# Layer 0's value products: sums of x by adding DMAs, sums of the weights on VectorE, later gathers, projections 8 steps ahead

## The chip, the cores and the metric

The kernel runs on one core of a Trainium2 chip. The metric is the device time of one execution in microseconds; the time of a kernel is the median of its timed runs. A profile is one further execution, recorded by the hardware profiler, with a time of its own.

The engines, as the profile abbreviates them: PE is TensorE (matmuls; PEld its weight loads), DVE is VectorE, ACT is ScalarE, POOL is GpSimd, SP is SyncE, which here only issues DMAs. Each engine executes its instructions in an order that is fixed when the kernel is built. An instruction that must wait holds up all behind it on its engine.

## The reference

Two layers of a decoder trunk over 1024 tokens of width 1024, in float32. Layer 0 mixes tokens by differential attention, layer 1 by forgetting attention; each is followed by a gated MLP with a short convolution, and residuals with LayerNorm. The change touches the attention of layer 0 only:

```python
q, k, v = jnp.split(x @ w_qkv, 3, axis=-1)           # 1024 x 1024 each
q = apply_rotary(q.reshape(B, S, H, 2, d), ...)      # 8 heads x 2 components x 64, 16 of 64 rotated
k = apply_rotary(k.reshape(B, S, H, 2, d), ...)
v = v.reshape(B, S, H, 2 * d)
# per block of 128 queries
s = einsum('bhcqd,bhckd->bhcqk', qb, k) * d ** -0.5
p = masked_softmax(s, causal_mask)
a = p[:, :, 0] - lam * p[:, :, 1]
o = einsum('bhqk,bhkd->bqhd', a, v)
o = rms_norm(o, subln_g) * (1.0 - lambda_init)
# all blocks together, then @ w_o
```

## The kernel before

**Number format.** Every large product is made of three matmuls (`mm3`, L104 to L106): each operand is cut into a high part and a remainder, and high x high, high x remainder and remainder x high are summed. `split` makes the two parts: an ACT copy (L91) for the high part and a DVE subtraction (L95) for the remainder.

**Loads and first projections.** `first_pair_rotary` loads x transposed (`in_xT`: 128 partitions x 8 blocks of the contraction x 1024 tokens) and the first two weight slabs, computes the rotary tables (their DMAs go through POOL's queue), and projects the query and key of head pair 0, first for tokens 0 to 511 (c = 0), then for 512 to 1023 (c = 1). `value_weights` (L379) loads all of the value weights, 8 tiles of 512 KB, on SP. `exp_table` loads ACT's table for the exponential in a section of its own.

**The value products.** `values_upfront` computes all values at once, x (1024 x 1024) times a 1024 x 1024 weight, by Winograd's form of Strassen's method: x and weight are taken as 2 x 2 blocks (halves of the tokens or features, `lo` and `hi`, and halves of the contraction, `k` and `H + k` with H = 4), and seven half-size products replace eight. Products 1, 2 and 4 use blocks of x as they are; 5, 7, 6 and 3 need sums of blocks:

- product 5: x(k, hi) + x(H+k, hi)
- product 6: that minus x(k, lo)
- product 7: x(k, lo) - x(k, hi)
- product 3: x(H+k, lo) minus the operand of product 6

The weights need sums of the same kind for 5, 6, 7 and 4. Before the change DVE makes the sums of x and POOL those of the weights (all by the helper `sub`, L411). Raw blocks of x come in by `load` (L403) into the tile `xs`, one per k, and `x1`, which has only two buffers of tag `wst`, so that the third and fourth are loaded after product 6 has used the first and second. `make(m, k)` produces the operands of product m for block k; `product` runs 4 row groups j of 12 matmuls per two k; `drain` combines PSUM results and stores the values to DRAM (L476), from where `load_values` (L533) reads them for each head pair. The products run in passes (1, 2), (5, 6), (7, 3), (4), in each pass k by k with the two products in turn, the last two k together. Operands are made up to `V_AHEAD` = 4 ahead.

**Rotation of pair 0.** The rotated rows are gathered by 12 small DMAs per half of the tokens (`gather`, L630 and L632) into the tile `rt`, multiplied by the tables (`turn`, L639 to L641, DVE), written back (L645) and then split (`halves`, with moves L273). All DMAs but the rotary tables' are issued by SP. `after(n, f)` defers f by n pulses; a pulse comes with every three matmuls of a product. Before the change the first half is gathered as soon as its projection is copied out, and its turn is called ahead of the second half's results.

**The attention loop.** For each of 8 head pairs (p), 16 score jobs run (two components j for each block qt of 128 queries: two groups of matmuls L682/L683, a masked minimum on DVE L685, the exponential on ACT L708, the normalisation L713, the combination on DVE L718), followed by transposes (L1544), value products and the norm of the heads (`diff_values`: squares summed by a matmul with ones, L743). Between jobs `step` advances the projection of later pairs by one block of the contraction, three matmuls per step. A pair's projection (`project_rotary`) is 4 quarters of 8 steps: (query, c=0), (key, c=0), (query, c=1), (key, c=1). `SHIFT` sets how far the projections run ahead: pair 0 advances them by 32 + SHIFT steps, pairs 1 to 5 by 32, pair 6 by 32 - SHIFT, and pair 7 has the output projection's first 64 steps instead. `ahead` (L113) loads a weight slab into a `wst` buffer, `ready` cuts it; the second component's exponentials use the `wst` buffers too, from qt = 4 on, and the free half of `rt` for qt < 4. `D_EV`, `D_ROT` and `D_CUT` are the delays of evacuation, turn and cut behind a quarter, in pulses.

Of the kernel before, what the change touches and what calls it, by code (L numbers as in the profile page):

```python
# [15 lines left out]
ALU = mybir.AluOpType  # L16
# [22 lines left out]
D_EV, D_ROT, D_CUT, D_TV = 1, (9, 10), ((14, 14), (18, 20)), 1  # L39
V_ROT, V_CUT, V_G, V_AHEAD = 20, (12, 32), 2, 4  # L40
SHIFT, D_VAL = 16, 10
# [17 lines left out]
class Trunk:  # L59
# [281 lines left out]
    def first_pair_rotary(self, t):  # L341
# [13 lines left out]
        for c in range(2):  # L355
# [3 lines left out]
            if c:  # L359
                self.turn(dst, r, 0)  # L360
# [4 lines left out]
            self.gather(dst, r, c)  # L365
        self.lam_exp()
        self.after(V_ROT, self.turn, dst, r, 1)
# [5 lines left out]
    def value_weights(self):  # L373
# [6 lines left out]
        return tiles[::2], tiles[1::2]  # L380

    def values_upfront(self, raw, cur):
# [6 lines left out]
        (g, u), H = raw, KT // 2  # L389
# [8 lines left out]
        xs, x1, ops = {}, {}, {}  # L398
        self.flip, n_s = False, 0

        def load(d, k, ns, t):
            d[k] = t
            nc.sync.dma_start(t.rearrange("p (k n) -> p k n", k=2), self.i["xT"][:, k:k + H + 1:H, ns])  # L403

        for k in range(H):
            load(xs, k, lo, self.tmp(pool=self.tt, tag="pt") if k < 3 else self.tmp(pool=self.pp, tag="p"))
            if k < 2:
                load(x1, k, hi, self.tmp(pool=self.wp, tag="wst", bufs=2))
# [4 lines left out]

        def make(m, k):
            nonlocal n_s
            gp, ve = nc.gpsimd, nc.vector
            if m == 5:
                sub(gp, g[k][:, lo], g[k][:, hi], g[k][:, lo])
                sub(ve, x1[k][:, hi], x1[k][:, lo], x1[k][:, hi], ALU.add)
                src = x1[k][:, hi]  # L420
            elif m == 6:
                sub(gp, g[k][:, lo], u[k][:, hi], g[k][:, lo])
                src = sub(ve, x1[k][:, hi], x1[k][:, hi], xs[k][:, lo])
            elif m == 7:
                sub(gp, g[k][:, hi], u[k][:, hi], g[k][:, hi])
                src = xs[k][:, lo]
            elif m == 3:
                src = xs[k][:, hi]
            elif m == 4:
                sub(gp, u[k][:, lo], u[k][:, lo], g[k][:, lo])  # L430
# [5 lines left out]
            else:  # L436
# [3 lines left out]
                self.split(*x, src)  # L440
                if m == 6:
                    sub(ve, xs[k][:, hi], xs[k][:, hi], src)
                    sub(ve, xs[k][:, lo], xs[k][:, lo], x1.pop(k)[:, lo])
                    if k < 2:
                        load(x1, k + 2, hi, self.tmp(pool=self.wp, tag="wst", bufs=2))
# [1322 lines left out]
```

## Time and profile before

| what | us |
|---|---|
| timed runs: median (lowest to highest of 3) | 2474.3 (2473.54 to 2485.29) |
| the profiled execution's own time | 2467.94 |
| its span | 2466.1 |
| mean granted clock of PE | 0.993 |
| the value products' matmuls (`wo`), first to last | 37.3 to 137.5 |
| windows of the head pairs, by their first scores: pair 0 | 138 to 185 |
| pair 1 | 185 to 232.5 |
| pair 6 | 413 to 465.2 |

How to read the rows of the profile: a row of a timeline has the start and the duration in us, engine, line, operation, output <- inputs, and in brackets the idle time before it with what ended it. A row of grouped instructions ends in busy us, mean ns of one, and idle time before them. A row of windows has the stretch, its length, the engine's busy time with its count of instructions, then for all engines alike PE's granted clock (1.00 is full speed), the mean busy share of the 16 DMA engines, and GB/s. A row of waits has total us, times, longest us. A row of DMA issues has the count, KB each, and the median us from issue to landing.

### The profile page before, as it was taken

The page shows a single profiled execution, that of the slowest core. Times are in us where ns is not written, and L with a number is a line of the kernel's source. Part 1 is how long each engine was busy: PE and PEld are TensorE (multiplying, and loading weights), DVE is VectorE, ACT ScalarE, POOL GpSimd, SP SyncE. Part 2 cuts the span into 40 slices and gives each one's busy share as a digit, 9 for nine tenths or more (in the row PEclk, how much of TensorE's full clock was granted, in tenths as well). Part 3 has the DMA queues.
Part 4 walks back from the last instruction along what each step waited for, and adds up shares of the span by engine and source line. Part 5 has one row for each costly group of instructions (what it writes and reads, how often), then busy time and mean ns, then how long its engine had stood idle before and what let it go on. Part 6 is the DMA issues. An engine that isn't in the chain of part 4 may idle for free.

```text
span 2466.1 us, 33746 instructions
## 1 busy us (share of the span) xinstructions
PE 2403.4 (97%) x11691; PEld 1998.3 (81%) x11691; DVE 1930.4 (78%) x3763; ACT 1312.5 (53%) x2516; POOL 163.7 (7%) x337
## 2 busy tenths in 40 slices
PE   7799999999999999999999999999999999999998
PEld 6588888778888888888778888888888888888886
DVE  5778888889867667887858777778898667668977
ACT  3467788766544444544535555555565444445444
POOL 4101111001000000000101000000010000000000
PEclk9899999999999999999999999999999999999999
DMA  6454335532322223975232222225223222328851
GB/s 198 150 164 130 107 98 144 162 107 94 103 77 77 94 86 98 337 253 171 87 99 62 67 66 65 65 74 171 78 86 111 78 77 78 97 97 318 270 170 69
DMA packets 140467, 304.38 MB, mean 123 GB/s; under 512 B 19116, under 2 KB 43564, under 8 KB 140296
## 3 DMA queue, kind: packets, MB, share of 16 engines
q1 hardware_dynamic: 139496, 300.32, 38.1%
q8 instruction: 92, 1.51, 0.3%
q0 software_dynamic: 800, 1.90, 0.2%
q14 instruction: 79, 0.65, 0.1%
HBM read 201.03 MB, written 67.57 MB: 109 GB/s over the span
## 4 chain that ended last, share of the span: by engine, by line
PE 78%; DVE 9%; ACT 6%; DMA 4%; issue 2%; SPq 1%; POOL 0%; DVEq 0%; ACTq 0%; POOLq 0%
PE m L104 19%; PE m L106 18%; PE m L105 18%; PE s L104 4%; PE s L105 4%; PE s L106 4%; PE m L1544 3%; PE s L683 2%; PE s L682 2%; PE m L1570 1%; PE m L1569 1%; DVE s L685 1%; DMA q<-q 1%; DMA t<-od 1%; DMA pt<-in_wd 1%
## 5 line engine op out<-in xcount | busy, mean ns | idle before, releaser
L104 PE MATMUL m<-xh,wh 128*128 128x512 f32 x640 | 266.7, 417 | 12.5 <-ACT xh L91 10.6
L104 PE MATMUL m<-xh,wo 128*128 128x512 f32 x656 | 255.9, 390 | 1.1 <-DVE xl L95 0.9
L106 PE MATMUL m<-xh,wo 128*128 128x512 f32 x656 | 255.6, 390 | 0.0
L105 PE MATMUL m<-xl,wo 128*128 128x512 f32 x656 | 255.6, 390 | 0.0
L106 PE MATMUL m<-xh,wl 128*128 128x512 f32 x640 | 253.8, 397 | 0.0
L105 PE MATMUL m<-xl,wh 128*128 128x512 f32 x640 | 252.4, 394 | 0.5 <-DVE xl L95 0.5
L91 ACT ACTIVATE wo<-wg 128x512 fp32r<-128x512 f32 x168 | 106.3, 633 | 223.7 <-PE m L106 215.8
L685 DVE CUSTOM_DVE_ANT_0 s<-s,mask 128x128 f32<-128x128 f32 (+7 forms) x256 | 194.0, 761 | 35.8 <-PE s L683 34.8
L104 PE MATMUL m<-q,wo 128*128 128x512 f32 x472 | 184.2, 390 | 0.0
L106 PE MATMUL m<-q,wo 128*128 128x512 f32 x472 | 183.9, 390 | 0.0
L105 PE MATMUL m<-q,wo 128*128 128x512 f32 x472 | 183.9, 390 | 0.0
L91 ACT ACTIVATE pt<-m 128x512 fp32r<-128x512 f32 (+1 forms) x240 | 128.6, 554 | 101.6 <-PE m L1544 67.4
L95 DVE TENSOR_TENSOR pt<-m,pt 128x512 fp32r<-128x512 f32 (+1 forms) x240 | 148.6, 633 | 23.3 <-ACT pt L91 20.5
L91 ACT ACTIVATE wo<-t 128x512 fp32r<-128x512 f32 x135 | 84.7, 627 | 142.3 <-PE m L106 134.8
L677 POOL CAST qz<-q 64x128 fp32r<-64x128 f32 x256 | 97.7, 383 | 847.5 <-PE s L683 774.5
L104 PEld LDWEIGHTS m<-xh,wh 128*128 128x128 f32 x640 | 121.6, 190 | 32.5 <-ACT xh L91 11.0
L95 DVE TENSOR_TENSOR wo<-wg,wo 128x512 fp32r<-128x512 f32 x168 | 115.5, 688 | 38.8 <-ACT wo L91 37.9
L104 PEld LDWEIGHTS m<-xh,wo 128*128 128x128 f32 x656 | 123.2, 188 | 27.2 <-PE m L1136 1.4
L105 PEld LDWEIGHTS m<-xl,wo 128*128 128x128 f32 x656 | 123.2, 188 | 25.5
L106 PEld LDWEIGHTS m<-xh,wo 128*128 128x128 f32 x656 | 123.2, 188 | 25.5
L106 PEld LDWEIGHTS m<-xh,wl 128*128 128x128 f32 x640 | 120.8, 189 | 26.1 <-DVE wl L95 0.6
L682 PE MATMUL s<-q,q 128*128 128x512 f32 (+3 forms) x384 | 134.0, 350 | 6.3 <-ACT p L708 4.2
(392 smaller groups left out, 6337.0 us busy)
## 6 DMA issues: line engine op xcount, KB each, us to landing
t<-in_wi SPq DMA_DIRECT2D x44, 512.0 KB
ha<-ad SPq DMA_DIRECT2D x88, 256.0 KB
wg<-in_wi SPq DMA_DIRECT2D x42, 512.0 KB
ad<-t SPq DMA_DIRECT2D x42, 512.0 KB
wst<-in_w SPq DMA_DIRECT2D x38, 512.0 KB
q<-q SPq DMA_DIRECT2D x128, 128.0 KB
pt<-in_wd SPq DMA_DIRECT2D x24, 512.0 KB
hb<-in_wd SPq DMA_DIRECT2D x44, 256.0 KB
```

Of the source, the lines that this page charges most:

```text
L91: i = nc.scalar.activation(hi, src, AF.Copy, scale=1.0 if scale is None else scale)
L95: nc.vector.tensor_tensor(lo, src, hi.bitcast(F32), op=ALU.subtract)
L104: mm(out, wh, xh, start=start, stop=False)
L105: mm(out, wh, xl, start=False, stop=False)
L106: mm(out, wl, xh, start=False, stop=stop)
L677: nc.gpsimd.tensor_copy(qz[r:r + 64, :], q[r:r + 64, qt * P:qt * P + P])
L682: nc.tensor.matmul(sb[:, ks], q[:, qt * P:qt * P + P], kd[:, ks], start=True, stop=False)
L683: nc.tensor.matmul(sb[:, ks], qz[rows], kl[rows, ks], start=False, stop=True)
L685: nc.vector.tensor_tensor_reduce(sb[:, :ln], sb[:, :ln], self.mask[:, S - ln:], 1.0, BIG, ALU.add, ALU.min, mn)
L1544: nc.tensor.transpose(tb[:, w:w + P], self.pts[q][:, kt * P:kt * P + P], k.ident)
L1569: mm(o, self.v[0][:, vs], h, start=first, stop=False)
L1570: mm(o, self.v[0][:, vs], l, start=False, stop=last)
```

## The change

- `value_weights` also loads the sums of x. For each k it makes three sums in place: a plain load by SP of one block, and then adding DMAs by POOL's queue, which read a block of `in_xT` from DRAM and add it onto the tile. `x1` lo gets (k, hi) + (H+k, hi), `x2` gets (k, hi) + (H+k, hi) + (k, lo), `x1` hi gets (k, lo) + (k, hi). These are 12 loads and 16 adds, 256 KB each. The loads are pinned behind the eight weight loads on SP, ahead of all gathers. Once product 6 has split its `x2`, one more adding DMA puts (H+k, lo) onto it for product 3 (4 in all).
- So that all sums of x are additions, the half of x for tokens 512 to 1023 is taken with its sign turned. Products 5, 6, 7 and 4 take their weights' sums with the sign that this asks for, and the drains for that half of the tokens scale by -1.
- The sums of the weights move from POOL to DVE. DVE's sums of x go.
- Pair 0's rotation is deferred: the gathers of the halves to 1 and 23 pulses, the turns to 20 and 42, the cuts to 31 and 54 (before: gathers at once, turns ahead of the second half's results and at 20, cuts at 12 and 32).
- In the loop `SHIFT` goes from 16 to 8; a quarter's gather is issued per operand; turns and cuts get new delays; the loads and cuts of weight slabs move to other quarters; in the last pair the second component's exponentials take other buffers; the matmul with ones is called a pulse later.

```diff
@@ -36,9 +36,9 @@
 
 AHEAD = 6
 EARLY = 8
-D_EV, D_ROT, D_CUT, D_TV = 1, (9, 10), ((14, 14), (18, 20)), 1
-V_ROT, V_CUT, V_G, V_AHEAD = 20, (12, 32), 2, 4
-SHIFT, D_VAL = 16, 10
+D_EV, D_ROT, D_CUT, D_TV = 1, (8, 8), ((14, 14), (14, 14)), 1
+V_ROT, V_GA, V_CUT, V_G, V_AHEAD = (20, 42), 19, (31, 54), 2, 4
+SHIFT, D_VAL = 8, 10
 W_CUT = 3
 D_V = 5, 9
 LAG, VLAG, W_C = 1, 0, 2
@@ -356,15 +356,15 @@
             ps = [self.mbank() for _ in range(2)]
             for _ in zip(*[self.dense_steps(ps[s], *self.w[s], c) for s in range(2)]):
                 pass
-            if c:
-                self.turn(dst, r, 0)
             for s in range(2):
                 self.result(0, 0, s, c, ps[s], dst[s], t)
             if c == 0:
                 self.exp_table()
-            self.gather(dst, r, c)
         self.lam_exp()
-        self.after(V_ROT, self.turn, dst, r, 1)
+        for c in range(2):
+            for j in range(2):
+                self.after(V_ROT[c] - V_GA, self.gather, dst, r, c, j)
+            self.after(V_ROT[c], self.turn, dst, r, c)
         for c in range(2):
             for j in range(2):
                 self.after(V_CUT[c], self.halves, dst, t, c, j)
@@ -377,7 +377,21 @@
         for n, t in enumerate(tiles):
             self.tc.keep_in_program_order(
                 self.nc.sync.dma_start(t, self.i["wv0"][n // 2 + n % 2 * 4]))
-        return tiles[::2], tiles[1::2]
+        H, lo, hi = KT // 2, slice(0, 512), slice(512, 1024)
+        x1 = [self.tmp(pool=self.wp, tag="wst", bufs=2) for _ in range(2)] + \
+            [self.tmp(pool=self.tt, tag="pt") for _ in range(2)]
+        x2 = [self.tmp(pool=self.tt, tag="pt"), self.tmp(pool=self.pp, tag="p")]
+        x2 = [t[:, ns] for t in x2 for ns in (lo, hi)]
+        for k in range(H):
+            for dst, parts in ((x1[k][:, lo], ((k, hi), (H + k, hi))), (x2[k], ((k, hi), (H + k, hi), (k, lo))),
+                               (x1[k][:, hi], ((k, lo), (k, hi)))):
+                for n, (kt, ns) in enumerate(parts):
+                    src = self.i["xT"][:, kt, ns]
+                    if n:
+                        self.nc.gpsimd.dma_start(dst, src, accum_op=ALU.add)
+                    else:
+                        self.tc.keep_in_program_order(self.nc.sync.dma_start(dst, src))
+        return tiles[::2], tiles[1::2], x1, x2
 
     def values_upfront(self, raw, cur):
 
@@ -386,7 +400,7 @@
 
 
         nc = self.nc
-        (g, u), H = raw, KT // 2
+        (g, u, *sums), H = raw, KT // 2
         lo, hi = slice(0, 512), slice(512, 1024)
         passes = ((1, 2), (5, 6), (7, 3), (4,))
         onto = {6: 1, 7: 1, 4: 1, 3: 5}
@@ -395,39 +409,27 @@
                            self.tp.tile([P, 1024], F32R, tag="t", name=self.nm("vs"))]
         c12 = [self.tmp(pool=self.pp, tag="p") for _ in range(4)]
         self.vd = [[self.dr.tile([8, P, 512], F32, name=f"vd{c}{f}") for f in range(2)] for c in range(2)]
-        xs, x1, ops = {}, {}, {}
+        x1, x2, ops = sums[0], sums[1], {}
         self.flip, n_s = False, 0
-
-        def load(d, k, ns, t):
-            d[k] = t
-            nc.sync.dma_start(t.rearrange("p (k n) -> p k n", k=2), self.i["xT"][:, k:k + H + 1:H, ns])
-
-        for k in range(H):
-            load(xs, k, lo, self.tmp(pool=self.tt, tag="pt") if k < 3 else self.tmp(pool=self.pp, tag="p"))
-            if k < 2:
-                load(x1, k, hi, self.tmp(pool=self.wp, tag="wst", bufs=2))
 
         def sub(eng, dst, x, y, op=ALU.subtract):
             eng.tensor_tensor(dst, x, y, op=op)
             return dst
 
+        def neg(dst, x, y):
+            nc.vector.scalar_tensor_tensor(dst, x, -1.0, y, op0=ALU.mult, op1=ALU.subtract)
+
         def make(m, k):
             nonlocal n_s
-            gp, ve = nc.gpsimd, nc.vector
+            ve = nc.vector
             if m == 5:
-                sub(gp, g[k][:, lo], g[k][:, hi], g[k][:, lo])
-                sub(ve, x1[k][:, hi], x1[k][:, lo], x1[k][:, hi], ALU.add)
-                src = x1[k][:, hi]
+                sub(ve, g[k][:, lo], g[k][:, lo], g[k][:, hi])
             elif m == 6:
-                sub(gp, g[k][:, lo], u[k][:, hi], g[k][:, lo])
-                src = sub(ve, x1[k][:, hi], x1[k][:, hi], xs[k][:, lo])
+                neg(g[k][:, lo], g[k][:, lo], u[k][:, hi])
             elif m == 7:
-                sub(gp, g[k][:, hi], u[k][:, hi], g[k][:, hi])
-                src = xs[k][:, lo]
-            elif m == 3:
-                src = xs[k][:, hi]
+                sub(ve, g[k][:, hi], u[k][:, hi], g[k][:, hi])
             elif m == 4:
-                sub(gp, u[k][:, lo], u[k][:, lo], g[k][:, lo])
+                neg(u[k][:, lo], g[k][:, lo], u[k][:, lo])
             w = {1: g[k][:, lo], 2: u[k][:, lo], 5: g[k][:, lo], 6: g[k][:, lo],
                  7: g[k][:, hi], 3: u[k][:, hi], 4: u[k][:, lo]}[m]
             if m in plain:
@@ -437,12 +439,9 @@
                 t = hold[n_s % 4]
                 n_s += 1
                 x = t[:, lo], t[:, hi]
-                self.split(*x, src)
+                self.split(*x, {5: x1[k][:, lo], 7: x1[k][:, hi], 6: x2[k], 3: x2[k]}[m])
                 if m == 6:
-                    sub(ve, xs[k][:, hi], xs[k][:, hi], src)
-                    sub(ve, xs[k][:, lo], xs[k][:, lo], x1.pop(k)[:, lo])
-                    if k < 2:
-                        load(x1, k + 2, hi, self.tmp(pool=self.wp, tag="wst", bufs=2))
+                    nc.gpsimd.dma_start(x2[k], self.i["xT"][:, H + k, lo], accum_op=ALU.add)
             self.flip = not self.flip
             bt = self.wp.tile([P, 1024], F32R, tag="wh" if self.flip else "wl", name=self.nm("wo"))
             self.split(bt[:, lo], bt[:, hi], w)
@@ -476,9 +475,9 @@
             nc.sync.dma_start(self.vd[c][f][j::4].rearrange("h p f -> p h f"),
                               t.bitcast(F32).rearrange("p (h f) -> p h f", h=2))
 
-        def parts(c, f, j, src):
+        def parts(c, f, j, src, scale=None):
             t = self.tt.tile([P, 1024], F32R, tag="pt", name=self.nm("vo"))
-            self.split(t[:, hi], t[:, lo], src)
+            self.split(t[:, hi], t[:, lo], src, scale)
             store(c, f, j, t)
 
         def drain(m, j):
@@ -492,11 +491,11 @@
                 self.split(t[:, hi].bitcast(F32R), t[:, lo].bitcast(F32R), t[:, lo])
                 store(0, 0, j, t)
             elif m == 4:
-                parts(1, 0, j, b)
+                parts(1, 0, j, b, -1.0)
             else:
                 h = hi if m == 7 else lo
                 sub(nc.vector, t[:, h], b, t[:, h], ALU.add)
-                parts(m == 7, 1, j, t[:, h])
+                parts(m == 7, 1, j, t[:, h], -1.0 if m == 7 else None)
 
         steps, makes, first = [], [], []
         for ms in passes:
@@ -539,12 +538,13 @@
 
         dst, r, i = [None] * 2, {"t": self.rt}, 2 * p
         for n, (s, c) in enumerate(((0, 0), (1, 0), (0, 1), (1, 1))):
-            if n == 2:
+            if n == 1:
                 self.ahead(i + 2)
-                self.after(1, self.ahead, i + 3)
                 self.after(5, self.ready, i + 2, True)
+            elif n == 2:
+                self.after(4, self.ahead, i + 3)
             elif n == 3:
-                self.after(2, self.ready, i + 3, True)
+                self.after(1, self.ready, i + 3, True)
             if p == NP - 1 and n > 1:
                 self.out_ahead(0, n - 2)
             ps = self.mbank()
@@ -552,8 +552,8 @@
             if c == 0:
                 dst[s] = self.tmp()
             self.after(D_EV, self.result, 0, p, s, c, ps, dst[s], t)
+            self.after(D_EV + (5 if n == 0 else 1), self.gather, dst, r, c, s)
             if s == 1:
-                self.after(D_EV + 1, self.gather, dst, r, c)
                 self.after(D_ROT[c], self.turn, dst, r, c)
                 for j in range(2):
                     self.after(D_CUT[c][j], self.halves, dst, t, c, j)
@@ -620,16 +620,16 @@
         else:
             self.split_k(0, 0, t, dst[1][:, sl], sl, True)
 
-    def gather(self, dst, r, c):
+    def gather(self, dst, r, c, j):
 
         t = r["t"][:, :512]
-        for j, x in enumerate(dst[:2]):
-            for h in range(2):
-                rows = 64 * j + 32 * h
-                n = slice(c * 512 + h * 256, c * 512 + h * 256 + 256)
-                self.nc.sync.dma_start(t[rows:rows + 32, :256], x[48:80, n])
-                for y in range(2):
-                    self.nc.sync.dma_start(t[rows + y:rows + 32:2, 256:], x[49 - y:80:2, n])
+        x = dst[j]
+        for h in range(2):
+            rows = 64 * j + 32 * h
+            n = slice(c * 512 + h * 256, c * 512 + h * 256 + 256)
+            self.nc.sync.dma_start(t[rows:rows + 32, :256], x[48:80, n])
+            for y in range(2):
+                self.nc.sync.dma_start(t[rows + y:rows + 32:2, 256:], x[49 - y:80:2, n])
 
     def turn(self, dst, r, c):
 
@@ -703,7 +703,8 @@
         sb, ln, mn = self.scores(0, t[j], t[2 + j], t[4], j, qt)
         lsum = self.small(tag="ls")
         yield
-        pt = self.tmp(pool=self.pp, tag="p") if j == 0 else self.rt[:, 512:] if qt < 4 else self.tmp() if last else \
+        pt = self.tmp(pool=self.pp, tag="p") if j == 0 else self.rt[:, 512:] if qt < 4 and not (last and qt % 2) else \
+            self.tmp() if last and qt > 2 else \
             self.tmp(pool=self.wp, tag="wst", bufs=2)
         nc.scalar.activation(pt[:, :ln], sb[:, :ln], AF.Exp, bias=mn, scale=-1.0, accum_out=lsum)
         yield
@@ -744,7 +745,7 @@
             nc.tensor.matmul(ms, self.ones, lo, start=False, stop=True)
             done.append(True)
 
-        self.after(1, sums)
+        self.after(2, sums)
         yield
         while not done:
             yield
```

## The prediction

> **What bounds the kernel now.** I read the page first, then TensorE (PE) stretch by stretch, then its waits, then the queues behind the longest wait.
>
> ```profile
> span 2466.1 us, 33746 instructions
> ...
> PE 2403.4 (97%) x11691; PEld 1998.3 (81%) x11691; DVE 1930.4 (78%) x3763; ACT 1312.5 (53%) x2516; POOL 163.7 (7%) x337
> ```
>
> PE is the bound, so only a stretch in which PE idles or runs slowly can give anything. The windows over layer 0's value stretch, and the same for tile `wo`, the operand of all value products:
>
> ```profile
> core 0: us, PE busy (x), PEclk, DMA share, GB/s
> 37.30:59.30 22.00, 22.00 (x97) 1.00 0.23 68
> 59.30:74.20 14.90, 0.05 (x1) 0.64 0.55 169
> 74.20:93.50 19.30, 18.37 (x66) 0.84 0.70 205
> 93.50:96.10 2.60, 0.02 (x2) 1.00 1.06 412
> 96.10:137.50 41.40, 41.40 (x175) 0.96 0.44 154
> ...
> 37.30:137.50 100.20, 81.81 (x336) 0.90 0.48 154
> ```
>
> The first row is PE undisturbed: 22.00 us / 97 = 0.227 us per matmul. 336 need 76.3 us; the stretch takes 100.2. So 23.9 us are lost: 18.4 idle (100.2 - 81.8), 5.5 by the lower clock after it (0.84 where PE restarts). The waits of PE before 200 us name the idle time (total, times, longest):
>
> ```profile
> PE m L104 <- DVE q L95: 14.9, 1, 14.9
> ...
> PE m L104 <- ACT q L91: 2.6, 1, 2.6
> ```
>
> PE waits for the split of the first sum of x. Behind it stand SyncE's queue (SP), then VectorE (DVE), both in order (start, duration):
>
> ```profile
> 47.68 0.61 SPq L403 DMA_DIRECT2D wst<-in_xT  x1
> 55.27 2.48 SPq L645 DMA_DIRECT2D t<-rt  x4
> ...
> 65.38 0.60 SPq L403 DMA_DIRECT2D pt<-in_xT  x1
> 66.02 0.61 SPq L403 DMA_DIRECT2D wst<-in_xT  x1
> ...
> 71.13 0.69 DVE L411 TENSOR_TENSOR wst<-wst 128x512 f32<-128x512 f32 x1 [2.54 <-DMA wst<-in_xT]
> ```
>
> SP stands from 48 to 55 us at `turn`'s write-back (L645), whose rows aren't rotated yet, then issues the other half's gathers, and only at 65.4 the rest of the loads of x. DVE stands at an add of the second sum until 71.1, with the split that PE wants behind it. This is head-of-line blocking, not bandwidth.
>
> The second loss is pair 6 of the attention loop (first PE, then DVE in the windows of single pairs, then one of PE's waits):
>
> ```profile
> 138.00:185.00 47.00, 47.00 (x239) 1.00 0.39 114
> 185.00:232.50 47.50, 44.42 (x250) 1.00 0.42 116
> ...
> 413.00:465.20 52.20, 46.09 (x253) 0.93 0.55 164
> ...
> 138.00:185.00 47.00, 33.50 (x87) 1.00 0.39 114
> 185.00:232.50 47.50, 38.32 (x102) 1.00 0.42 116
> ...
> PE s L682 <- ACT p L708: 3.5, 2, 3.2
> ```
>
> Pair 0 has 48 steps of projection to cover its softmax, and PE never idles; pair 6 has 16, and PE idles 6.1 us of 52.2, with clock lost too (0.93).
>
> **The change, part by part.**
>
> *Sums of x.* DVE loses 16 additions and subtractions, and gets the weights' 16 from GpSimd (POOL): the kinds cost the same, 16 x 0.68 = 11 us each way. POOL gets 16 adding DMAs ahead of the stretch and 4 behind product 6's splits, SP 12 plain loads; all move 256 KB.
>
> ```profile
> L411 DVE TENSOR_TENSOR pt<-pt,wst 128x512 f32<-128x512 f32 x6 | 4.0, 682 | 0.0
> ...
> L95 DVE TENSOR_TENSOR wo<-vw,wo 128x512 fp32r<-128x512 f32 x7 | 9.8, 1467 | 0.2 <-ACT wo L91 0.2
> ...
> L95 DVE TENSOR_TENSOR wo<-vw,wo 128x512 fp32r<-128x512 f32 x6 | 4.1, 686 | 0.3 <-ACT wo L91 0.3
> ```
>
> The x7 row is 36.7 to 46.4 us, beside POOL's additions; the x6 row is 101 to 118, without them. So with them gone DVE gains 7 x 0.78 = 5.5 us. PE is covered there: I count it as slack, not as gain.
>
> When do the sums arrive? SP's loads follow eight weight loads of 512 KB; the rates below are of windows, last column GB/s:
>
> ```profile
> 25.83 0.46 SPq L379 DMA_DIRECT2D t<-in_wv  x1
> ...
> 30.00:35.00 5.00, 0.00 (x0) 1.00 1.02 361
> 35.00:40.00 5.00, 2.33 (x2) 1.00 0.32 125
> ...
> 35.36 0.35 DVE L166 TENSOR_TENSOR sp<-sp 128x64 f32<-128x64 f32 x2
> ...
> rope<-rs POOLq DMA_DIRECT2D x2, 128.0 KB, 6.4
> rc<-of POOLq DMA_DIRECT2D x4, 32.0 KB, 3.6
> ```
>
> The queue is full to 35 us and moves 0.63 MB more (125 GB/s x 5 us), so it empties near 37; the first load of x (0.26 MB at 361 GB/s = 0.7 us) lands at 38. SP stands before the second load, whose slot the lambda products at 35.4 still read, until 36: beside a full queue that costs nothing. On POOL each k issues four adds of about 0.53 us; only the second of x2 must wait until the first has landed. If a link (issue to landing) takes L, a round takes L + 1.6 us, and x2's last sum is there at 38.5 + 3(L + 1.6) + 2L = 43.3 + 5L. No adding DMA is in the trace. Nearest rows: POOL's DMAs land after 3.6 us (32 KB) and 6.4 (128 KB beside a full queue): 61 and 75 us. PE, undisturbed, finishes products 1 and 2 at 59.3 and takes 2.72 us (12 x 0.227) per k and product, product 5 and 6 in turn; it wants x2[3] at 76.2, its splits 2 us before. So up to L = 6.2 nothing is late, at 6.4 about 1 us. I take L = 5, between the rows: last sum at 68, nothing late. Range of this term: the whole 23.9 us gained, or down to less than nothing (rivals). Some loss stays, since the order of DVE and ACT is fixed ahead and an early split may stand before a weight's: I take 4 us. **Value stretch: -20.**
>
> The 4 late adds wait for product 6's splits (from about 58 us); behind them POOL has only the copies `qz` of the first pair, wanted at the stretch's end. Product 3 needs them more than 20 us later: nothing.
>
> [...]
>
> ```profile
> 19.87 1.59 POOL L223 DMA_DIRECT2D rs<-of x3
> ...
> 16.41 4.91 DVE L95 TENSOR_TENSOR xl<-p,xh 128x512 fp32r<-128x512 f32 x8
> ```
>
> Three issues in 1.59 us, 0.53 each, while DVE splits without a gap.
>
> [...]
>
> *Rotation.* Gathers go to 1 and 23 pulses, turns to 20 and 42, cuts to 31 and 54, a pulse being 3 matmuls or 0.68 us. The last cut falls at about 37 + 54 x 0.68 = 74 us; the first scores come at 138, after the change near 118: covered. SP's wait at L645 now has no load of x behind it.
>
> *Projections 8 steps ahead, not 16.* Pair 6 gets 24 steps, pair 0 gets 40. Eight steps are 24 x 0.227 = 5.4 us of cover. In pair 6 they meet 6.1 us of idle time and slow clock behind it: **-5** (0 to -8). Pair 0 would have 41.6 us for DVE's 33.5, the ratio (0.81) of the next pair (38.3 of 47.5), which idles 3.1: **+1.5** (0 to +3). The second half's cut comes at step 24 + 14, six steps into the next pair, where before it came at 34 to 36; keys of that half are wanted at step 11 of 32 (weights 3 to 6 of 52 in all, 35%), five steps or 7 us later. Enough in long pairs, scarce in pair 6: **+1** (0 to +6; the weight load moved beside the exponentials' buffers is in it).
>
> *`sums` a pulse later.* It meets this wait (200 to 480 us):
>
> ```profile
> PE m L743 <- DVE sq L736: 1.6, 5, 0.8
> ```
>
> **-1** (0 to -1.6). The other buffers of the last pair and the two signs in the drains cost nothing that a row shows.
>
> **Sum**: -20 - 5 + 1.5 + 1 - 1 = -23.5 us. The profiled execution took 2467.94 us (span 2466.1), so 2444.4 by its own time. The three timed runs lie higher, median 2474.3, lowest 2473.54; from that median the sum gives **2451** us.
>
> **The rivals.**
>
> 1. *Sums half late.* L between 7 and 10 us, or in-order blocking on DVE: x2[3] at 78 to 93 us, 4 to 19 late; the gain of the stretch shrinks to 5 to 16: 2458 to 2470, centre 2464. For it: 6.4 us is in the trace. Against: that was beside a full queue, and after 45 us the queue is empty.
> 2. *Slower: the chain of adds on POOL is the bound.* Two links and three rounds follow one another whatever the bandwidth. DVE and POOL double each other's time when they overlap (1467 against 686 ns); 6.4 us doubled is L = 13: x2[3] at 108 us, 34 late, and 4 us more of clock. The stretch is 14 longer, less 3.5 from the rest: 2485. It decides from L = 11 (24 us late) on. Against: the rs row above.
> 3. *Nothing in the end.* The loop takes back what the stretch gives (late cuts, +2 us in each of 7 pairs), or ACT's section with the exponential's table waits for the adds as it now waits for POOL's last DMAs:
>
> ```profile
> 31.52 1.28 ACT L232 ACT_TABLE_LOAD   x1 [11.80 <-DMA rope<-rs]
> ```
>
> Adds landing until 65 us would hold ACT, which makes every weight split, for some 25 us, about the whole gain: 2470 to 2478. Against: the adds wait for loads that SP issues only after 26 us, when ACT is already in that wait.
>
> **How the numbers follow.** Half a per cent, 12.4 us, is about what a measurement can tell here. Forecast 0.62 (2441 to 2460, all faster). Rival 1 has 0.20: 0.08 faster, 0.12 within. Rival 2 has 0.10: 0.08 slower, 0.02 within. Rival 3 has 0.08, all within. Together 0.70 faster, 0.22 same, 0.08 slower. The range goes from 2440 (all 23.9 + 8 + 1.6 gained) to 2470 and leaves out rival 2 and most of rival 3, 0.17.
>
> **What would show it.** Right: no PE wait over 3 us between 59 and 97, the 336 `wo` matmuls in 76 to 82 us, adds landing 3 to 6 us after issue, pair 6 with under 2 us idle. Wrong: PE waiting on a split of x whose releaser is a DMA to `pt`, `p` or `wst` from POOL's queue; ACT's table load later than 31.5; new waits `s L682 <- DMA q<-q` in pairs 1 to 6.

## The result, and the profile after

| what | before | after |
|---|---|---|
| timed runs: median (lowest to highest), 4 each | 2477.7 (2473.54 to 2485.29) | 2456.62 (2453.93 to 2457.38) |
| the profiled execution's own time | 2467.94 | 2456.67 |
| its span | 2466.1 | 2454.7 |
| `wo` matmuls, first to last | 37.3 to 137.5 | 42.3 to 132.4 |
| loop: end of the value products to the first MLP matmul | 467.9 | 459.5 |

The ratio is 0.991, with a 95% interval of 0.9881 to 0.9938: 21.1 us faster by the medians (15 to 29 by the interval). The prediction was 2451 (2440 to 2470). Unrounded it was 2450.8; of the 5.8 us from there to 2456.6, 3.4 are the base (before's median rose from 2474.3 to 2477.7 with a fourth run) and 2.4 the forecast (-23.5 against -21.1).

By the two profiled executions the gain is only 11.3 us. A second profile of the kernel before (below) took 11.0 us longer than the first: its value products started 6.3 us later and its loop took 3.9 more. So a difference of that size between two single profiles proves nothing here; where it matters, I compare gains against runs of before on the same chip.

The profile page after, its lines on the span and the busy times:

```profile
span 2454.7 us, 33776 instructions
...
PE 2401.8 (98%) x11691; PEld 1996.5 (81%) x11691; DVE 1919.9 (78%) x3763; ACT 1311.7 (53%) x2516; POOL 159.0 (6%) x341
```

Windows of PE over the value stretch after, then pairs 0 and 6 (columns as before):

```profile
core 0: us, PE busy (x), PEclk, DMA share, GB/s
42.30:64.60 22.30, 22.27 (x97) 0.99 1.02 191
64.60:68.60 4.00, 1.99 (x7) 1.00 0.96 158
68.60:85.30 16.70, 16.68 (x71) 1.00 0.74 165
85.30:98.60 13.30, 7.96 (x29) 0.83 0.84 229
98.60:132.40 33.80, 33.80 (x137) 0.91 0.64 204
42.30:132.40 90.10, 82.70 (x338) 0.94 0.80 195
133.10:174.40 41.30, 41.30 (x214) 1.00 0.42 121
400.80:451.80 51.00, 44.91 (x257) 1.00 0.56 165
```

The wait of 14.9 us on a sum of x is gone: product 5 starts at 64.9 instead of 74.3. But the stretch is 90.1 us long where 76.3 would do and some 80 were forecast. Two holes remain, a small one at 64.6 to 68.6 (4.0 us for 7 matmuls, worth 1.6: 2.4 lost) and a large one at 85 to 99. There 5.3 us are idle, and the lower clock costs more behind it: 7.96 us busy for 29 matmuls (6.6 at 0.227) and 33.8 for 137 (31.1). Together 5.3 + 1.4 + 2.7 = 9.4 us. The waits of PE ahead of 133 us name both:

```profile
PE s L104 <- ACT p L486: 3.1, 1, 3.1
PE s L106 <- DVE vs L95: 2.2, 1, 2.2
PE m L104 <- DVE p L416: 1.7, 2, 1.5
```

*The large hole* belongs to SP's queue. ACT's timeline, with what ended the idle time in brackets, and SP's:

```profile
91.41 0.59 ACT L488 COPY p<-m 128x512 f32<-128x512 f32 x1 [4.76 <-DMA vd<-p]
...
95.39 0.58 ACT L488 COPY p<-m 128x512 f32<-128x512 f32 x1 [2.41 <-DMA vd<-p]
```

```profile
66.60 1.30 SPq L475 DMA_DIRECT2D vd<-p  x2
68.81 5.30 SPq L645 DMA_DIRECT2D t<-rt  x4
74.17 0.99 SPq L630 DMA_DIRECT2D rt<-t  x1
...
83.41 0.53 SPq L273 DMA_DIRECT2D q<-q  x1
...
88.04 0.58 SPq L475 DMA_DIRECT2D vd<-p  x1
...
89.31 0.78 SPq L475 DMA_DIRECT2D vd<-p  x1
```

ACT evacuates product 5 into tiles `p` whose old content, product 2's values, must first be stored (L475). SP issues the last two stores only at 88 and 89: ahead of them stand the write-back of the first half (L645), all 12 gathers of the second half and the moves L273. It is an in-order queue again, but not the same wait: SP stood 7 us at L645 before and only 0.8 now. It stands 12.2 us (54.4 to 66.6) at the first of the stores, until DVE has the values, and then the issuing of the write-back, the gathers and the moves takes it from 68.8 to 88.0.

*The small hole* belongs to the adds. They land 5.1 us after issue in the median, so L = 5 was right, but they don't run freely beside one another. DMA issues by POOL, and PE, DMA share and GB/s in two windows ahead of the hole:

```profile
pt<-in_xT POOLq DMA_DIRECT2D x10, 256.0 KB, 5.1
p<-in_xT POOLq DMA_DIRECT2D x6, 256.0 KB, 5.1
wst<-in_xT POOLq DMA_DIRECT2D x4, 256.0 KB, 6.2
```

```profile
45.00:55.00 10.00, 10.00 (x46) 8.28 (x45) 7.63 (x13) 3.79 (x7) 3.97 (x5) 1.00 1.01 193
55.00:65.00 10.00, 9.64 (x44) 7.69 (x42) 4.23 (x8) 4.43 (x9) 4.82 (x6) 1.00 0.99 152
```

The last two columns: all DMA engines are busy (1.01, 0.99) while they move 193 and 152 GB/s; a window before the change shows 412 GB/s at the same share. The first add lands at 47.6 and the seventeenth, x2[3], at 78.4: 30.8 / 16 = 1.9 us each (1.8 up to the fourteenth at 70.6, the last three further apart, while stores and write-backs go too). Never more than three are under way. ACT meets this at 61.5, where the split of x2[1] stands ahead of the weights' splits and of the evacuations that DVE then makes up for in a rush:

```profile
61.49 0.63 ACT L91 ACTIVATE vs<-pt 128x512 fp32r<-128x512 f32 x1 [3.57 <-DMA pt<-in_xT]
```

*The loop.* Pair 0 takes 41.3 us (46.8 before), pairs 1 to 5 226.4 (228.0), pair 6 51.0 (52.2 before, with 8 steps less to do then), from pair 7 to the MLP 140.1 (140.1). Pair 0 lost just the 5.4 us of its 8 steps, without any idle time; pair 6 took them on and still became shorter. Over the whole loop, before and then after:

```profile
137.50:605.40 467.90, 450.41 (x2409) 0.99 0.41 122
...
132.40:591.90 459.50, 445.19 (x2408) 1.00 0.41 124
```

For the same matmuls PE is busy 5.2 us less, of which the slow clock of pair 6 before (0.93 over 46.1 us) is some 3, and idle 3.2 us less (17.5, then 14.3). In pair 6 the idle time did not go: 52.2 - 46.1 = 6.1 us before, 51.0 - 44.9 = 6.1 after; what went there is the slow clock (0.93, then 1.00). PE's waits in the loop after:

```profile
PE s L682 <- DMA q<-q: 3.3, 4, 1.5
PE m L1545 <- DVE p L719: 1.8, 4, 0.9
PE m L1545 <- DVE pt L95: 1.7, 3, 1.2
PE s L682 <- DMA q<-t: 1.4, 3, 0.6
```

The scores' wait on the exponentials (L708, 3.5 us before) has fallen to 1.1 (L709 here); the other waits of pair 6 are ahead of transposes, on DVE (2.3), on the copy L607 (1.2) and on moved rows (1.1).

### The profile page after: what moved, and what is told of

Read it like the earlier page. It is cut to its first block, busy times and chain, and to the rows that moved or that the text cites. A ratio compares the mean times of both kernels' runs of the same rounds, so it can differ in the third digit from the quotient of the medians.

```text
span 2454.7 us, 33776 instructions
## 1 busy us (share of the span) xinstructions
PE 2401.8 (98%) x11691; PEld 1996.5 (81%) x11691; DVE 1919.9 (78%) x3763; ACT 1311.7 (53%) x2516; POOL 159.0 (6%) x341
## 3 DMA queue, kind: packets, MB, share of 16 engines
q0 software_dynamic: 3680, 7.15, 1.5%
## 4 chain that ended last, share of the span: by engine, by line
PE 76%; DVE 10%; DMA 7%; ACT 4%; issue 2%; SPq 1%; DVEq 0%; POOL 0%; ACTq 0%; POOLq 0%
PE m L104 18%; PE m L106 18%; PE m L105 18%; PE s L104 4%; PE s L105 4%; PE s L106 4%; PE m L1545 3%; PE s L683 2%; PE s L682 2%; PE m L1571 1%; DMA pt<-in_wd 1%; PE m L1570 1%; DMA q<-q 1%; DVE wo L95 1%; DVE s L685 1%
```

## The experiments

Gains are medians against before's on the same chip, since before itself lies between 2475.9 and 2478.2 on them. The changed kernel's is 21.1; its interval, 15 to 29 us, goes into every difference from it.

**The two parts alone.** The first run has the kernel before with the loop's edits only, the second the changed kernel with the loop's old settings:

```diff
 # e1: before, and
-SHIFT, D_VAL = 16, 10
+SHIFT, D_VAL = 8, 10
-D_EV, D_ROT, D_CUT, D_TV = 1, (9, 10), ((14, 14), (18, 20)), 1
+D_EV, D_ROT, D_CUT, D_TV = 1, (8, 8), ((14, 14), (14, 14)), 1
...
 # e2: after, and the reverse of these
```

> The kernel before with the loop's edits alone (projections 8 steps ahead instead of 16, new delays of gather, turn and cut, weight loads in other quarters, other buffers in the last pair, the matmul with ones a pulse later); the value stretch as before. Theory A, the loop as forecast: 4.5 us faster than before. Theory B, as the two profiles read (end of the value products to the first MLP matmul, 8.4 us shorter after the change): 8 to 9 us faster, with pair 6 (its first scores to those of pair 7) at about 51 us with 8 steps more in it. Theory C, the stretch's earlier end makes the loop's gain: no gain alone. The value products (first to last matmul) stay at 100 us in all three.

> The changed kernel with the loop's edits undone; the value stretch as changed. If the parts add up as in the two profiles: about 5 us faster than before (the value products 10 us shorter, their start 5 us later), about 8 us slower than the changed kernel. If the timed runs of before (6 to 17 us above its profiled one) lose more time in the stretch than its profile showed: 12 us or more faster than before. Value products 88 to 92 us, first one near 42 us if the late start comes from the change, near 37 if it was chance.

The loop alone: 2467.1 against 2476.05, ratio 0.996 (0.9946 to 0.9974), 9.0 us. The stretch alone: 2465.44, ratio 0.9964 (0.9951 to 0.9976), 10.6 us. They add up to 19.6 of 21.1. The loop is thus worth more than twice the 3.5 us of my sum and the stretch half of the 20. In e1 the loop takes 459.3 us, as after, and the stretch, which nothing touched, 96.9: with 100.2 and 98.5 in the traces of before that is its spread. In e2 the stretch takes 91.6 and the loop's old waits are there (L708 3.5 us, L743 2.6).

**SP's queue against the adds.** One run puts off the second half's gathers and turn; the other has the changed kernel's order and loads the same blocks without adding:

```diff
 # e3
-V_ROT, V_GA, V_CUT, V_G, V_AHEAD = (20, 42), 19, (31, 54), 2, 4
+V_ROT, V_GA, V_CUT, V_G, V_AHEAD = (20, 74), 19, (31, 86), 2, 4
 # e4
-self.nc.gpsimd.dma_start(dst, src, accum_op=ALU.add)
+self.nc.gpsimd.dma_start(dst, src)
```

> The changed kernel with the second half of pair 0's rotation later: turn at 74 pulses instead of 42, gather at 55 instead of 23, cut at 86 instead of 54, so that the four stores of product 2's results stand ahead of the second half's gathers on SyncE. Theory Q (queue order: after 85 us TensorE waits for copies that wait for those stores, which SyncE issues at 88 and 89 us behind twelve gathers): the idle time of 5.3 us between 85 and 99 us and the slow clock after it go, the value products take 80 to 84 us instead of 90, the whole is 6 to 9 us faster than the changed kernel. Theory T (throughput: the adding DMAs keep the DMA engines full from 45 to 75 us and everything behind them is late whatever its place): the stall stays, moved by under 3 us, the whole within 2 us.

> The changed kernel with its 20 adding DMAs issued as plain loads by the same queue at the same places: the additions are left out, so sums of x hold one block only. Theory T: these loads take 0.6 to 0.9 us each of the DMA engines instead of 1.75, the queue is empty by 60 us instead of 75, SyncE's gathers and stores come some 10 us earlier and the value products take 78 to 83 us instead of 90. Theory Q: the stores still stand behind the second half's gathers; the stall after 85 us stays within 2 us of 5.3, the value products take 86 us or more. The landings, issue to semaphore, show what the addition itself costs: 4.4 to 5 us with it.

The later rotation: 2449.76, ratio 0.9899 (0.9882 to 0.9915), 26.3 us. In its trace SP issues the two stores at 73.8 and 78.4, ahead of the gathers, and the large hole is gone (windows of PE: the hole's place, then the stretch):

```profile
73.83 1.09 SPq L475 DMA_DIRECT2D vd<-p  x1
...
78.39 0.37 SPq L475 DMA_DIRECT2D vd<-p  x1
...
82.62 0.59 SPq L630 DMA_DIRECT2D rt<-t  x1
```

```profile
85.00:99.00 14.00, 14.00 (x62) 1.00 0.71 179
40.10:122.80 82.70, 78.08 (x338) 1.00 0.84 208
```

Without that order there is no hole: undoing it alone takes the stretch from 90.1 to 82.7. Of these 7.4 us the timed medians show 5.2, which their intervals (15 to 29 and 21 to 29) do not set apart.

Without the additions (one run; its sums hold one block only) the time is 2442.72, the stretch takes 78.1 us, and PE has a single wait of 1.4 us in it although SP's order is the changed kernel's. SP reaches the first stores at 62.2 instead of 66.6 and the last two at 78.5 and 80.3. So both are causes of the large hole: the adds make the splits late and fill the DMA engines, which delays everything on SP, and the order then decides who pays. The same 20 transfers as plain loads, in the windows of 45 to 65 us:

```profile
45.00:55.00 10.00, 10.00 (x45) 8.26 (x45) 8.59 (x15) 3.99 (x8) 4.31 (x8) 1.00 0.95 323
55.00:65.00 10.00, 10.00 (x46) 8.27 (x45) 7.72 (x15) 6.89 (x12) 2.68 (x5) 1.00 0.76 256
```

The first lands at 46.0 and the eighteenth at 62.8, 1.0 us apart in the mean, for 1.9 with additions.

**Before once more.** No edit.

> The kernel before, profiled once more. Its timed runs lie near 2476, its profiled execution took 2467.9 and is the quickest of all; the changed kernel's profiled execution lies on its own median. If the profiled execution of before was a lucky one, this trace has a span of 2472 to 2479 and shows where the 6 to 10 us come and go (places outside the stretch and pairs 0 and 6, for instance single waits in the second layer); if the profiler itself makes before quicker, the span is again near 2466. Either way the value stretch should be 100 us within 1, starting at 37 within 2.

Its profiled execution took 2478.89 us (span 2477.1): value products 43.6 to 142.1 (98.5 us), loop 471.8. The start is 6.3 us later than in the first trace, the loop 3.9 longer. The start hangs in part on ACT's section with the exponential's table, which, as the profile has it, waits until DMAs under way have landed. The row of ACT's table load here, then after:

```profile
36.50 1.28 ACT L232 ACT_TABLE_LOAD   x1 [16.25 <-DMA t<-in_wv]
```

```profile
34.23 1.28 ACT L232 ACT_TABLE_LOAD   x1 [13.70 <-DMA vw<-in_wv]
```

In the first trace it waited for `rs` and came at 31.5; here a load of the weights held it until 36.5, with no adding DMA in the kernel. The start was 40.4 in e1, which has the stretch of before, and 39.0 in e2, which has the changed one. So a start as late as 42.3 comes without the change too. The start and the stretch here both lie outside what I expected (37 within 2, 100 within 1). Against this trace, the span is 22.4 us shorter after: 1.3 start, 8.4 stretch, 12.3 loop, and 0.4 in what follows.

**The table early.**

```diff
+        self.exp_table()
...
-            if c == 0:
-                self.exp_table()
```

The first line stands right behind the rotary tables; the two small copies go to a tile of their own.

> The changed kernel, with ACT's exponential table loaded right behind the rotary tables instead of between the halves of pair 0's projection, and its two small copies into a tile of their own, so that they do not wait for the tables' DMAs. Theory S: the value products start at 42.3 instead of 37.3 because ACT's section with the table load waits for DMAs under way (13.7 us up to the table load at 34.2); then the first product falls to 34 to 38 us and the time by 3 to 6 us, to 2451 to 2454. Rival: the start is set by the DMA queue that brings the weights (loads of x and of the adds now stand among them), then the start stays at 40 to 42 and the time within 2 us of 2456.6.

2453.3, ratio 0.9908 (0.9892 to 0.9925), 22.6 us: against the changed kernel's 21.1 not told apart. The expectation compared with 2456.6 from another chip, which made the gain look like 3.3. The table came at 24.4 but the products started only at 40.0, where the rival had them: PE is busy without a gap from 30 us on. So the section is not all that sets the start.

**Product 7's sums last.** The four sums for product 7 are loaded and added behind all others.

```diff
-        for k in range(H):
-            for dst, parts in ((x1[k][:, lo], ...), (x2[k], ...), (x1[k][:, hi], ...)):
+        for ks, late in ((range(H), False), (range(H), True)):
+            for dst, parts in [(x1[k][:, hi], ((k, lo), (k, hi))) for k in ks] if late else \
...
```

> The changed kernel with the four sums x(k, lo) + x(k, hi), wanted only by product 7, loaded and added behind all others; nothing else is changed. Theory T (the adds go through one at a time, about 1.75 us each, whatever is asked): two adds ahead of x2[1] and one ahead of x2[0] go, so x2[1] lands 3 to 4 us earlier (from 65 to about 61), x2[3] from 78.4 to about 72, and the waits of PE at 64.9 and 68.5 (1.9 us) go or fall under 0.5; the waits at 85 to 99 stay, since they belong to SP's queue. The time falls by 1 to 3 us. Rival (a link's latency sets the sums, not the throughput): x2[1] lands within 1 us of 65 and the waits stay.

2453.3, ratio 0.9909 (0.9894 to 0.9924), 22.6 us, again not told apart. The sum that ACT waits for came at 60.1 instead of 61.5, not the 3 to 4 us earlier that I expected, since only one add fewer went ahead of it. The wait at 64.9 went, that at 68 stayed (1.2).

**Half of the builder's `dynamic_dma_scratch_size`.**

```diff
-    nc = bacc.Bacc("TRN2", ..., dynamic_dma_scratch_size=1024)
+    nc = bacc.Bacc("TRN2", ..., dynamic_dma_scratch_size=512)
```

> The changed kernel with half of the space for POOL's DMA descriptors (512 instead of 1024 in the builder's argument); nothing else is changed. In the changed kernel never more than three adding DMAs are under way, and one lands each 1.75 us. Theory R (the descriptor space limits how many are under way): with half of it one, seldom two, are under way, one lands each 2.5 to 5 us, x2[3] lands behind 90 us, the stretch grows by 10 us or more. Rival (the engines that add are the limit, and a third one under way only waits): landings stay at 1.6 to 2.0 us apart and the time within 3 us of 2456.6.

2484.59 (one run; before's median 2475.92 on that chip). PE's waits in its stretch, and two windows of all engines:

```profile
PE m L104 <- ACT wo L91: 20.6, 1, 20.6
PE s L104 <- ACT vs L91: 13.9, 2, 13.3
```

```profile
55.00:65.00 10.00, 10.00 (x45) 8.07 (x43) 1.39 (x2) 0.63 (x2) 2.01 (x3) 1.00 0.37 53
65.00:75.00 10.00, 0.16 (x1) 0.00 (x0) 0.69 (x1) 1.59 (x3) 2.43 (x3) 0.72 0.36 52
```

One add at a time: each lands 4.3 us after issue in the median and the next is issued as it lands. One lands each 4.6 us (59.8, 64.4, 69.0), and the engines are busy 0.37 of the time: 0.37 x 4.6 = 1.7 us of all engines for an add, near the 1.9 us at which they land with three under way. So with 512 one add was under way and with 1024 three, and with three the engines' share was 1.01 and 0.99. That more than 1024 would gain little is my estimate from these shares; it was not tried. In e4, with 1024, plain loads landed 4.3 us after issue in the median (3.1 to 7.7) and 1.0 us apart, by which some four were under way. POOL's queue counts 144 packets for an add and 80 for a plain load of the same size (3680, 2400 and 800 packets in all after, in e4 and before, for 20 transfers); what of them the setting limits was not shown. The stretch grew to 118.8 us.

**What in the loop.** SHIFT back to 16 in the changed kernel, first with the new delays, then with the old ones as well:

```diff
 # e9 and e12
-SHIFT, D_VAL = 8, 10
+SHIFT, D_VAL = 16, 10
 # e12 too
-D_EV, D_ROT, D_CUT, D_TV = 1, (8, 8), ((14, 14), (14, 14)), 1
+D_EV, D_ROT, D_CUT, D_TV = 1, (9, 10), ((14, 14), (18, 20)), 1
```

> The changed kernel with SHIFT back at 16 (pair 0 does 48 steps of projection, pair 6 does 16); the shorter delays, the gathers per operand and the moved weight slabs stay. Theory P: the loop's gain of 8 to 12 us is pair 6's cover, so the wait of scores on the exponential's normalisation comes back in pair 6 (about 4 us in all, with the lower clock behind it) and the loop goes from 459.5 to 464 to 468, the time to 2461 to 2465. Rival: the gain comes from the delays and buffers; then pair 6 keeps short waits, the loop is within 3 us of 459.5 and the time within 3 us of 2456.6.

> The changed kernel with SHIFT at 16 and the old delays of turn and cut (9, 10 and 14, 14, 18, 20); the gathers per operand, the moved weight slabs and buffers and the later squares' sum stay. With SHIFT 16 and the new delays the loop took 475.0 us, 15.5 more than in the changed kernel: each pair 1 to 5 took 46 us for 44, and transposes waited for DVE's splits in all pairs, 6 above all. If the short delays are what SHIFT 16 cannot bear (DVE's turn and cut meet the softmax of the same steps), the pairs 1 to 5 come back to about 45 us, the loop to 466 to 471 as before the change, the time to 2461 to 2466, with pair 6 still waiting. If SHIFT alone makes the gain and the delays are neutral, the loop stays at 472 to 475 and the time at 2466 to 2470. If the buffers and slabs were the gain, the loop goes to 459 to 463, the time to 2456 to 2460.

2468.54, ratio 0.9957 (0.9941 to 0.9974), and 2471.63, ratio 0.9977 (0.9966 to 0.9989): gains of 9.7 and 5.6, loops of 475.0 and 476.3 us. So the 8 steps are worth 11.4 us in this kernel (21.1 - 9.7, with an interval of some 8 us either way), the whole gain of the loop; the traces of the loop, 475.0 against 459.5, say the same. Without them the other edits show no gain, and the shorter delays are, if anything, good. But the place is not the one that I named: pairs 1 to 5 take 236.0 us in e9 (226.4 in the changed kernel), pair 6 50.0 with 5.4 us less to do (51.0). Nor are the waits: with the new delays PE waits for splits and combinations ahead of transposes, 10.7 us in pairs 1 to 5 and as below in pair 6, and with the old ones a value product waits 0.8 to 2.3 us for a split in every pair from 1 to 5. PE's waits in pair 6 of e9, then from pair 1 to the end of pair 5 of e12:

```profile
PE m L1545 <- DVE p L719: 2.7, 1, 2.7
PE m L1545 <- DVE pt L95: 2.5, 2, 2.2
```

```profile
PE m L104 <- DVE pt L95: 8.0, 5, 2.3
```

Why DVE falls behind there by just so much is not settled. SHIFT 8 alone in the kernel before was not tried.

**Together.** The later rotation and product 7's sums last, with the table early (e10) and without (e11):

> The changed kernel with three of the edits tried so far together: the second half's rotation at 74 and 86 pulses, the exponential's table right behind the rotary tables, product 7's sums last. Alone against the changed kernel's 2456.6 they gave -6.9, -3.3 and -3.3 us. If each removes a wait of its own (SP's queue, ACT's section, the adds' order) they add up: 2443 us, the value products in 78 to 81 us from a start at 40 or earlier, and no wait of PE above 1.5 us between 60 and 115. If the waits stand for one another, the sum is that of the largest alone, 2447 to 2450.

> As the run with all three edits, but with the exponential's table left where the changed kernel has it. If ACT's table section costs what it cost alone, this run is 2 to 4 us slower than the one with all three, with the start of the value products at 40 to 43.5 us, changing from one execution to the next; if the start was chance alone, the two agree within 1 us.

2448.28 (2445.49 to 2453.5), ratio 0.988 (0.9863 to 0.9897), and 2447.36 (2446.28 to 2448.26), ratio 0.9874 (0.9859 to 0.9888). Of the kernels whose sums are whole, the second has the lowest median: 30.9 us under before on the same chip, with a stretch of 79.5 us. The 2443 of the expectation was added up from medians of different chips. By gains on the same chip the three edits are worth 5.2 + 1.5 + 1.5 us beyond 21.1, together 29.3, and e10 has 30.0: they add up within the noise, which is larger than two of the three. Moving the table gave nothing on top, and the traces suggest why. Its products started at 38.6, e11's at 43.7, but the sums of x land at the same times, so that e10 waits for them where e11 hardly does (PE's waits, e10 from 20 to 123 us):

```profile
PE m L104 <- DVE p L417: 4.8, 2, 4.0
```

Product 5 begins at 64.6 in the one and 65.7 in the other. In these two traces, the arrival of the sums is the bound, not the start.

## Why the prediction was right, and where it was not

The total was right, -23.5 against -21.1, but that is luck, by two errors that cancel: the stretch gave 7 to 11 us (6.8 to 10.1 in traces, 10.6 in e2's timed runs) instead of 20, the loop 8 to 12 instead of 3.5. Of the four signs of being right only one came, links of 3 to 6 us (5.1 in the median). PE waited 3.1 us at 85 to 97, the `wo` matmuls took 90.1 us instead of 76 to 82, and pair 6 idles 6.1 us instead of under 2. Two signs of being wrong came: a split of x held by a DMA of POOL's queue (61.5), and ACT's table load at 34.2, which comes so late without the change too.

- **Links of 5 us: right. Arrival of the last sum at 43.3 + 5L: wrong.** L was 5.1, which gives 68.8; x2[3] landed at 78.4. The step that failed is the round of L + 1.6 us in which adds cost only latency. They share the engines and landed 1.9 us apart. The sum also left out the 12 plain loads of x: it had the queue empty near 37, with the first sum at 38.5 + L, but the queue was still full from 35 to 45 us, and the first add was issued at 40.2 and landed at 47.6 (rows below). Of the 9.6 us that x2[3] was late, 4.0 are this later beginning and 5.6 the slower pace. By itself this cost little: 2.4 us at 64 to 69, within the 4 us that I had set aside for splits standing ahead of weights' splits, the mechanism that took place.

```profile
35.00:40.00 5.00, 3.32 (x7) 0.61 1.04 394
40.00:45.00 5.00, 5.00 (x17) 0.70 1.07 347
```

- **"SP's wait at L645 now has no load of x behind it": true, and not enough.** I asked which loads stand behind the moved rotation, not which stores. Product 2's last two stores stood behind it, its gathers and its moves, and that cost 9.4 us. With them ahead (e3) the stretch is 82.7 us long, 17.5 less than in the first trace of before: nearly the 20 of the forecast. Without the additions (e4) it is 78.1.
- **Covered rotation: right for its end, wrong on the way.** Keys and queries of pair 0 were in time; the DMAs that make them weren't free.
- **Pair 6, -5: right in size, not in mechanism.** Its window fell by 1.2 us with 5.4 us more of projection in it, 6.6 gained. But the steps did not fill its idle time, which is 6.1 us before and after; the wait on L708 fell from 3.5 to 1.1 us and others took its place. What shows in its window is the clock (0.93, then 1.00); some of its work now also falls behind its end (676 matmuls from there to the MLP before, 694 after).
- **Pair 0, +1.5: wrong.** Its window shows no idle time with 40 steps. A ratio of DVE's work to the window (0.81) like the next pair's did not mean idle time like the next pair's.
- **The pairs between, not in the sum.** 1.6 us less than in the first trace, 3.8 against the second (230.2). That, pair 6 and pair 0 make the loop's surplus, some 1.6 us each against the first trace.
- **Late cuts, +1; squares' sum, -1.** Waits of scores on moved rows (`q<-q`, `q<-t`) come to 4.7 us, more than I priced; the wait on squares fell from 1.6 us to 0.5, as priced.
- **Weights' sums on VectorE: right.** The weights' subtractions take 691 ns each in 25 of them, where 7 had taken 1467.
- **Rival 1** was half there: sums late by 10 us and splits blocking in order, but on ACT, and a gain of the stretch within its 5 to 16 us; most of the loss came by SP's stores, though. **Rival 2**: that the chain of adds can be the bound shows in e8, but not by its mechanism. There a link took 4.3 us, not 13, one add ran at a time, and x2[3] landed at 120.8, not 108; that the time, 2484.6, meets the 2485 worked out is chance. (The row that it rests on showed the doubling for DVE's splits only: POOL's subtractions took 1.61 to 1.74 us beside them, at 37.6 to 51.1 us, and some 1.30 at 63.4 to 66.0, where DVE was idle nearly throughout.) In the changed kernel three run at once, and it did not come about. **Rival 3** fell: the loop gave and did not take, and ACT's table section waits as long without adds (16.25 us in e5, 13.70 after).
- **POOL's issue of 0.53 us: right for plain DMAs, short for adds.** Before the change POOL issued three in 1.59 us beside DVE's splits and two in 1.03 with DVE idle (at 24.6 us), and in e4 one of the plain loads in 0.54. An adding DMA took 0.87 us to issue, beside the splits and sums that DVE runs here, and links stayed near 5 us.

## What to carry to other kernels

Before moving a wait on an in-order queue, list everything that the queue issues behind it, the stores that free buffers as well as the loads. Count an adding DMA by its engine time, not by its latency alone (here 1.9 us from landing to landing, 5.1 from issue to landing), and place plain traffic that others need soon ahead of it. Test parts one at a time even when the total comes out as forecast.

## What the runs showed of the hardware that was not expected

- An adding DMA of 256 KB took 1.7 us of all 16 engines in e8 (0.37 x 4.6) and 1.9 from landing to landing in the changed kernel, over twice a plain load's in e4 (0.262 MB at 323 GB/s and a share of 0.95: 0.8 us; 1.0 from landing to landing). POOL's issue took 0.87 us against 0.54.
- How many of them were under way changed with the builder's `dynamic_dma_scratch_size`: three with 1024, one with 512 (e8). Of plain loads some four were under way with 1024, by 4.3 us to land and 1.0 us apart.
- ACT's section with a table load was held by DMAs under way, 11.8 to 16.3 us in the traces of before and after, and the start of the value products moved between 37.3 and 43.6 us in two executions of the same kernel.
